# In the mixer, each group's sample step takes its sixteen small products in two runs, by operand height, instead of in turns head by head

## The chip, the cores and the metric

The kernel runs on one core of a Trainium2 chip. The time is the device time of one execution in microseconds (us). A profile of one execution gives the start and duration of every instruction on the engines: PE (TensorE, matmuls), PEld (the weight loads of PE), DVE (VectorE), ACT (ScalarE), POOL (GpSimd), and SP, which issues most DMAs.

## The reference

One step of a streaming encoder: two layers, 512 frames of a new stream (the prompt) and 32 frames of a running stream (the sample), which share all weights. The first layer holds a Mamba-2 mixer, the second a stick-breaking attention; both have two SwiGLU blocks around them. The part that matters here is the mixer's scan, in chunks; the prompt has four chunks of 128 frames in this kernel, the sample is one chunk of 32, and the sample alone starts from a carried state:

```python
cb = jnp.einsum('bign,bjgn->bijg', C_c, B_c)
y_diag = jnp.einsum('bijg,bijge,bjgep->bigep', cb, decay, x_c)
y_off = jnp.einsum('bign,bgepn->bigep', C_c, state) * jnp.exp(a_cs)[..., None]
...
new_state = state * jnp.exp(a_cs[:, -1])[..., None, None] + jnp.einsum(
    'bjgn,bjge,bjgep->bgepn', B_c, w_end, x_c)
return new_state, y_diag + y_off
```

There are 4 groups of 8 heads, 64 columns to a head and 128 states.

## The kernel before

All 544 frames go through the dense products together, as two halves of 272 columns. A dense product is written as three (high and low parts), so that PE runs long rows of `mm` matmuls of 128x128 weights on 272 columns. In the mixer (function `mamba`) the scan of a group g in 0 to 3 and chunk c in 0 to 4 (c = 4 is the sample) is cut into steps that are squeezed in between those dense rows: `turn_x` and `turn_b` (transposes, tiles `xd`, `xw`, `btok`), `decay` and `decay_ab` (tiles `ex`, the decays times C·B, and `ab`, the decays times C), `state` (new state, tile `st`), and `output`.

`output` holds the two products of a head: `xd`ᵀ`ex` (the y_diag term; its operands have as many rows as the chunk has frames: 128, or 32 for the sample) and `st`ᵀ`ab` (the y_off term; 128 rows, one for each state). Both add up in the same place of a PSUM tile `py`. Eight heads share that tile: heads 2t and 2t+1 lie at columns t·128 on, the even one on partitions 0 to 63 (PE's left column half) and the odd one on 64 to 127 (the right half). In the profile's rows the first product is `aux<-ex,xd` and the second `aux<-ab,st`; a form such as 32\*64 is the height and width of the part of PE that the instruction uses. Each of these fp32 products is two instructions on PE.

What follows what on each engine is set by a planner (class `Plan`): each step is a chain that yields requests with a price ("T", 1.2, ... is 1.2 us on PE), and the planner emits whichever can start earliest by its own prices and lags. The engines then keep that order. So a changed price changes the order of everything that the planner places later. The last step of a group's `y` then goes through `gnorms` to the output product (`mm<-yh`, `mm<-yl`).

Of the kernel before, what the change touches and what calls it, by code (L numbers as in the profile page):

```python
# [10 lines left out]
P = 128  # L11
# [4 lines left out]
T = TP + TS  # L16
# [28 lines left out]
NZB, NY, NYH = 1, 2, 4  # L45

RGNORM, RSCAN, RCONV, RGATE, ROUT, RSTEP = 39, 4, 20, 45, 2, 41

FIRST = [0, 1, 2, 3], [0, 1, 2, 3], [0, 1, 2, 3], [0, 1, 2, 3]
GROUPS = [(4, 5), (6, 7)], [(8, 9), (10, 11)], [(12, 13), (14, 15)], [(16, 17), (18, 19), (20, 21)]  # L50
# [126 lines left out]
def v_cost(n):  # L177
    return n / 960.0 + 0.069


def _body(tc, io):
# [17 lines left out]
    V, S, G, TE = (Engine(n, e) for n, e in (("V", nc.vector), ("S", nc.scalar), ("G", nc.gpsimd), ("T", nc.tensor)))  # L199
# [4 lines left out]
    with ExitStack() as ctx:  # L204
# [767 lines left out]
        def mamba(norm, after, ready, ahead):  # L972
            with tc.tile_pool(name="mt", bufs=1, reuse_waits="tile") as tmp, \
# [6 lines left out]
                def aux():  # L980
                    return pa.tile([P, 512], F32, tag="aux", name="aux")
# [8 lines left out]
                got = {}  # L990
# [292 lines left out]
                def before(c):  # L1283
                    return "s" if c == 4 else c - 1
# [33 lines left out]
                def output(g, c):  # L1318
                    off, n = chunks[c]
                    src = off if c < 4 else SOFF  # L1320
                    xs = got["x", g]
                    need = [("ex", g, c), ("xd", g, c), ("xw", g, c), ("cd", g, c)]
                    yield "wait", *need
                    if c > 0:
                        yield "wait", ("st", g, before(c))
                    if c == 0:
                        yield "get", "y"
                        got["y", g] = tmp.tile([P, 4, T], F32, tag="y", name="y", bufs=NY)
                        yield "set", ("y0", g)
                    else:  # L1330
                        yield "wait", ("y0", g)
                    yield "get", "aux"
                    py = aux()
                    xd, ex, ab = got["xd", g, c], got["ex", g, c], got["ab", g, c]

                    def emit(t):
                        for b in range(2):
                            h = 2 * t + b
                            dst = py[64 * b:64 * b + 64, t * P:t * P + n]
                            TE.matmul(dst, xd[:n, h, :], ex[:n, h, :], start=True, stop=c == 0)  # L1340
                            if c > 0:
                                TE.matmul(dst, got["st", g, before(c)][:, h, :], ab[:, h, :], start=False, stop=True)
                    for t in range(4):
                        yield "T", (1.2 if n < P else 0.87) if c else 0.44, lambda: emit(t)
                    yield "set", ("y", g, c)
                    yield "put", "ex"
                    yield "put", "xd"
                    yield "put", "ab"
                    pyv = py[:, :].rearrange("p (t i) -> p t i", t=4)[:, :, :n]
                    yv = got["y", g][:, :, off:off + n]  # L1350

                    def skip(t):
                        V.scalar_tensor_tensor(out=yv[:, t], in0=xs[:, t, src:src + n], scalar=dskip[:, 4 * g + t:4 * g + t + 1], in1=pyv[:, t],
                                               op0=ALU.mult, op1=ALU.add)
                    for t in range(4):
                        yield "W", v_cost(n) + 0.06, lambda: skip(t)
                    yield "put", "aux"
                    yield "set", ("out", g, c)

                def ssd(g):  # L1360
                    yield "wait", "tok", *[("in", g, t) for t in range(6)]
                    if g > 0:
                        yield "wait", ("ex", g - 1, 4), ("xd", g - 1, 4)
                    for c in range(5):
                        yield "spawn", turn_x(g, c)
                        yield "spawn", turn_b(g, c)
                        yield "spawn", decay(g, c)
                        yield "spawn", state(g, c)
                        yield "spawn", output(g, c)
                        if c < 4:  # L1370
                            yield "wait", ("ex", g, c)
                        if c == 2:
                            yield "spawn", old_state(g)
                    yield "wait", *[("out", g, c) for c in range(5)], ("st", g, 4)
                    yield "put", "grp"
# [545 lines left out]
        def space(name, side=None):  # L1921
            st = ExitStack()
            return st, st.enter_context(tc.tile_pool(name=name, bufs=1, reuse_waits="tile", **({"side": side} if side else {})))
# [5 lines left out]
        st, tmp = space("ff")  # L1929
# [34 lines left out]
        st, tmp = space("pl")  # L1964
# [12 lines left out]
        st, tmp = space("ff")  # L1977
# [8 lines left out]
        st, tmp = space("pl")  # L1986
# [145 lines left out]
```

## Time and profile before

| | us |
|---|---|
| median of 3 runs | 2303.37 (2301.47 to 2303.8) |
| the profiled execution | 2301.52 |
| its span, first to last instruction | 2299.8 |
| PE busy | 2267.0 (99%) |
| DVE busy | 1680.0 (73%) |
| ACT busy | 1011.1 (44%) |
| POOL busy | 575.7 (25%) |

An instruction counts as busy from its start to its end, and matmuls overlap, so a busy PE is not PE at its peak: what one matmul costs is read from the time between the starts of two. The profile also gives the clock that was granted to PE in a stretch, as a share of 2.4 GHz: 1.00 is 2.4 GHz and 0.50 is 1.2 GHz.

### The profile page before, as it was taken

To read this page: it belongs to the slowest core of one execution; us is meant where nothing else is said; L and a number is where in the kernel's file an instruction comes from. 1 tells how busy PE (TensorE), PEld (TensorE's weight loads), DVE (VectorE), ACT (ScalarE), POOL (GpSimd) and SP (SyncE) were. 2 spreads that over 40 slices of the span, in tenths; PEclk is the share of its full clock that TensorE was granted. 3 is DMA by queue.
4 is the path that set the end of the run, shared out by engine and by line. 5 is a ranking of instruction groups with operands and counts; after the bars stand their busy time and mean duration, and the time that the engine had idled before them with its cause. 6 is when DMAs were issued, how large, how long until landed. Compare 5 with 4: busy or idle time off the path is not lost.

```text
span 2299.8 us, 42811 instructions
## 1 busy us (share of the span) xinstructions
PE 2267.0 (99%) x17937; PEld 2207.0 (96%) x17937; DVE 1680.0 (73%) x2201; ACT 1011.1 (44%) x1489; POOL 575.7 (25%) x541
## 2 busy tenths in 40 slices
PE   9999999999999999999999999999998999999997
PEld 9999999989899999999999999999985899999997
DVE  7777786679777676777757767778678576777857
ACT  5333334567646353333345533333468353333343
POOL 1221122244324122121221122121234122221224
PEclk9999999999999999999999999999999999999999
DMA  5233323333433232333232423332311132333232
GB/s 170 85 91 106 97 67 90 112 100 94 110 97 99 75 119 79 106 93 106 65 99 91 130 81 104 100 98 65 89 45 56 47 117 86 92 106 97 67 100 76
DMA packets 111537, 213.19 MB, mean 93 GB/s; under 512 B 12400, under 2 KB 33520, under 8 KB 111344
## 3 DMA queue, kind: packets, MB, share of 16 engines
q1 hardware_dynamic: 108464, 204.92, 29.7%
q10 hardware_dynamic: 2880, 5.53, 0.7%
q8 instruction: 141, 2.31, 0.4%
q14 instruction: 52, 0.43, 0.1%
HBM read 204.83 MB, written 5.60 MB: 91 GB/s over the span
## 4 chain that ended last, share of the span: by engine, by line
PE 92%; DVE 4%; ACT 2%; issue 1%; POOL 1%; DMA 1%; SPq 0%; DVEq 0%; ACTq 0%; POOLq 0%
PE mm L193 82%; PE z L193 3%; PE aux L193 3%; PE o L193 1%; PE f L193 1%; PE tr L193 1%; DVE wlo L193 1%; ACT whi L193 1%; DVE xl L193 1%; POOL ab L193 0%; DVE x L193 0%; DVE e L193 0%; DMA wraw<-in_wpg 0%; DVE fu L193 0%; DVE rm L193 0%
## 5 line engine op out<-in xcount | busy, mean ns | idle before, releaser
L193 PE MATMUL mm<-xh,whi 128*128 128x272 f32 x2096 | 513.0, 293 | 2.3 <-DVE x L193 1.0
L193 PE MATMUL mm<-xh,wlo 128*128 128x272 f32 x2096 | 506.2, 289 | 1.8 <-DVE wlo L193 1.8
L193 PE MATMUL mm<-xl,whi 128*128 128x272 f32 x2096 | 507.7, 290 | 0.3 <-DVE xl L193 0.3
L193 PEld LDWEIGHTS mm<-xh,whi 128*128 128x128 f32 x2096 | 358.6, 189 | 10.5 <-issue 7.2
L193 PEld LDWEIGHTS mm<-xh,wlo 128*128 128x128 f32 x2096 | 358.3, 189 | 2.3 <-DVE wlo L193 2.2
L193 PEld LDWEIGHTS mm<-xl,whi 128*128 128x128 f32 x2096 | 358.3, 190 | 0.7 <-DVE xl L193 0.7
L193 ACT ACTIVATE whi<-wraw 128x1024 fp32r<-128x1024 f32 (+3 forms) x215 | 184.2, 858 | 374.5 <-PE mm L193 263.3
L193 PE MATMUL mm<-xfh,whi 128*128 128x272 f32 x1152 | 332.4, 289 | 0.0
L193 PE MATMUL mm<-xfl,whi 128*128 128x272 f32 x1152 | 332.3, 288 | 0.0
L193 PE MATMUL mm<-xfh,wlo 128*128 128x272 f32 x1152 | 332.2, 288 | 0.0
L193 DVE TENSOR_TENSOR wlo<-wraw,whi 128x1024 fp32r<-128x1024 f32 (+3 forms) x252 | 257.0, 1020 | 72.6 <-ACT whi L193 54.6
L193 PE MATMUL mm<-hh,whi 128*128 128x272 f32 x1408 | 291.5, 288 | 0.0
L193 PE MATMUL mm<-hh,wlo 128*128 128x272 f32 x1408 | 291.1, 288 | 0.0
L193 PE MATMUL mm<-hl,whi 128*128 128x272 f32 x1408 | 290.9, 288 | 0.0
L193 ACT ACTIVATE whi<-a 128x1024 fp32r<-128x1024 f32 x127 | 134.9, 1062 | 319.8 <-PE mm L193 214.4
L193 DVE TENSOR_TENSOR wlo<-a,whi 128x1024 fp32r<-128x1024 f32 x145 | 178.4, 1230 | 101.7 <-ACT whi L193 67.2
L193 PEld LDWEIGHTS mm<-hl,whi 128*128 128x128 f32 x1408 | 221.5, 189 | 0.0
L193 PEld LDWEIGHTS mm<-hh,whi 128*128 128x128 f32 x1408 | 221.2, 188 | 0.0
L193 PEld LDWEIGHTS mm<-hh,wlo 128*128 128x128 f32 x1408 | 220.7, 189 | 0.0
L193 PEld LDWEIGHTS mm<-xfh,wlo 128*128 128x128 f32 x1152 | 217.1, 188 | 0.0
L193 PEld LDWEIGHTS mm<-xfl,whi 128*128 128x128 f32 x1152 | 217.1, 188 | 0.0
L193 PEld LDWEIGHTS mm<-xfh,whi 128*128 128x128 f32 x1152 | 217.1, 188 | 0.0
(290 smaller groups left out, 4108.0 us busy)
## 6 DMA issues: line engine op xcount, KB each, us to landing
a<-in_wgu SPq DMA_DIRECT2D x145, 512.0 KB, 3.9
wraw<-in_wd SPq DMA_DIRECT2D x128, 256.0 KB, 2.7
wraw<-in_win SPq DMA_DIRECT2D x41, 512.0 KB, 3.6
wraw<-in_wgu SPq DMA_DIRECT2D x29, 512.0 KB, 3.7
wraw<-in_wd SPq DMA_DIRECT2D x32, 384.0 KB, 3.1
ab<-acs_d SPq DMA_DIRECT2D x16, 512.0 KB, 4.7
wraw<-in_wout SPq DMA_DIRECT2D x16, 512.0 KB, 3.6
wraw<-in_wpg SPq DMA_DIRECT2D x16, 512.0 KB, 3.6
```

Source lines behind the costliest of these rows:

```text
L193: ins = getattr(self.engine, op)(*args, **kw)
```

## The change

For the sample, the step `emit` (a pair of heads, each `ex` product followed by its `ab` product; four such steps) gives way to one step `emit_sample`: all eight heads' `ex` products, then all eight heads' `ab` products. Only the first two of them (t = 0, one in each column half) carry the flag that starts a new sum in the tile. The planner's price for a group's sample step goes from 4 times 1.2 to 1.8. The other four chunks keep their code and prices.

```diff
+TSSD = 0.44, 0.87
...
-                    for t in range(4):
-                        yield "T", (1.2 if n < P else 0.87) if c else 0.44, lambda: emit(t)
+                    def emit_sample():
+
+                        for old in range(2):
+                            for h in range(8):
+                                t, b = divmod(h, 2)
+                                dst = py[64 * b:64 * b + 64, t * P:t * P + n]
+                                if old:
+                                    TE.matmul(dst, got["st", g, before(c)][:, h, :], ab[:, h, :], start=False, stop=True, skip_group_check=True)
+                                else:
+                                    TE.matmul(dst, xd[:n, h, :], ex[:n, h, :], start=t == 0, stop=False, skip_group_check=True)
+                    if n < P:
+                        yield "T", 1.8, emit_sample
+                    else:
+                        for t in range(4):
+                            yield "T", TSSD[c > 0], lambda: emit(t)
```

On PE, at the sample step of group 0, the order before goes on like this for eight heads (one row is one product):

```order
L193 MATMUL mm<-xh_4143,wlo 128x272 x2
L193 MATMUL aux<-ex,xd 64x32
L193 MATMUL aux<-ab,st 64x32
L193 MATMUL aux<-ex,xd 64x32
L193 MATMUL aux<-ab,st 64x32
L193 MATMUL aux<-ex,xd 64x32
```

and now it is this, at the same place between the same dense products:

```order
L195 MATMUL mm<-xl_4144,whi 128x272 x2
L195 MATMUL mm<-xh_4143,wlo 128x272 x2
L195 MATMUL aux<-ex,xd 64x32 x8
L195 MATMUL aux<-ab,st 64x32 x8
L195 MATMUL mm<-xh_4190,whi 128x272 x2
```

The sixteen products have become two runs of eight; up to this place nothing on PE has moved.

Behind that, the planner's order differs. At the sample step of group 2, before, PE had these rows after the last prompt chunk's state product (`xw,btok`), thirty more rows of dense products, and then the sample's products in turns:

```order
L193 MATMUL aux<-C,B 32x32
L193 MATMUL aux<-xw,btok 128x512
L193 MATMUL mm<-yh,whi 128x272 x2
L193 MATMUL mm<-yl,whi 128x272 x2
L193 MATMUL mm<-yh,wlo 128x272 x2
```

Now the sample's products stand three rows of dense products behind it:

```order
L195 MATMUL aux<-xw,btok 128x512
L195 MATMUL mm<-yh,whi 128x272 x2
L195 MATMUL mm<-yl,whi 128x272 x2
L195 MATMUL mm<-yh,wlo 128x272 x2
L195 MATMUL aux<-ex,xd 64x32 x8
L195 MATMUL aux<-ab,st 64x32 x8
```

In the mixer as a whole, the dense rows are broken by scan products 56 times now, 53 times before.

On POOL, whose product `ab<-ab,C` the sample's second run reads, group 2 had this before (the `whi` row is a weight's high part, copied for the dense products):

```order
L193 TENSOR_TENSOR st<-st,fade 128x512
L193 TENSOR_TENSOR xw<-xd,tok 32x512
L193 TENSOR_SCALAR whi<-wraw 128x1024
L193 TENSOR_TENSOR ab<-ab,C 128x256
L193 TENSOR_TENSOR st<-st,fade 128x512
L193 TENSOR_TENSOR yl<-y,yh 128x544
```

and has this now:

```order
L195 TENSOR_TENSOR st<-st,fade 128x512
L195 TENSOR_TENSOR xw<-xd,tok 32x512
L195 TENSOR_TENSOR ab<-ab,C 128x256
L195 TENSOR_TENSOR st<-st,fade 128x512
L195 TENSOR_SCALAR yh<-y 128x544
```

The copy of the weight has left that place of POOL's queue.

## Rows read from the trace of the kernel before

**Rows 1.** Page: busy time of each engine; the chain that ended last, by engine.

```profile
PE 2267.0 (99%) x17937; PEld 2207.0 (96%) x17937; DVE 1680.0 (73%) x2201; ACT 1011.1 (44%) x1489; POOL 575.7 (25%) x541
PE 92%; DVE 4%; ACT 2%; issue 1%; POOL 1%; DMA 1%; SPq 0%; DVEq 0%; ACTq 0%; POOLq 0%
```

**Rows 2.** The mixer: length, busy time of PE, PEld, DVE, ACT, POOL; clock; DMA.

```profile
424.00:760.00 336.00, 332.54 (x2710) 309.75 (x2710) 248.94 (x448) 206.37 (x347) 121.45 (x138) 0.98 0.34 100
```

**Rows 3.** Whom PE waited for, 400 to 860: us in total, times, longest.

```profile
PE aux L193 <- POOL ab L193: 1.2, 2, 0.9
PE aux L193 <- POOL xw L193: 0.9, 1, 0.9
PE aux L193 <- DVE btok L193: 0.8, 1, 0.8
PE mm L193 <- DVE wlo L193: 0.7, 1, 0.7
```

**Rows 4.** PE's order of time, group 2's sample: start, us, instruction, count.

```profile
633.44 0.30 PE L193 MATMUL aux<-ex,xd 32*64 32x32 f32 x2
633.66 0.30 PE L193 MATMUL aux<-ab,st 128*64 128x32 f32 x2
...
636.87 0.30 PE L193 MATMUL aux<-ab,st 128*64 128x32 f32 x2
637.10 0.52 PE L193 MATMUL mm<-yh,whi 128*128 128x272 f32 x2
```

**Rows 5.** The same, cut fine: first pair's second matmul, its two weight loads.

```profile
633.52 0.22 PE L193 MATMUL aux<-ex,xd 32*64 32x32 f32 x1
633.43 0.13 PEld L193 LDWEIGHTS aux<-ex,xd 32*64 32x64 f32 x1
633.49 0.13 PEld L193 LDWEIGHTS aux<-ex,xd 32*64 32x64 f32 x1
```

**Rows 6.** PE cut fine (0.02 and 0.01 us), then whole: runs of one form.

```profile
1766.03 0.33 PE L193 MATMUL o<-an,vt 32*64 32x128 f32 x2
543.14 0.33 PE L193 MATMUL aux<-ex,xd 128*64 128x128 f32 x2
543.14 1.09 PE L193 MATMUL aux<-ex,xd 128*64 128x128 f32 x16
```

**Rows 7.** Stretches, PE alone: length, busy time and instructions, granted clock, DMA.

```profile
489.00:492.40 3.40, 3.40 (x31) 1.00 0.30 107
492.40:495.81 3.41, 3.41 (x16) 0.50 0.59 159
495.81:499.20 3.39, 3.39 (x29) 1.00 0.00 0
633.44:637.10 3.66, 3.66 (x33) 1.00 0.36 140
637.10:640.50 3.40, 3.40 (x29) 1.00 0.51 153
584.56:587.97 3.41, 3.41 (x15) 0.50 0.58 154
```

**Rows 8.** PE and POOL in order of time, sample steps of groups 0 and 3.

```profile
487.78 0.30 PE L193 MATMUL aux<-ex,xd 32*64 32x32 f32 x2
488.94 0.30 PE L193 MATMUL aux<-ab,st 128*64 128x32 f32 x2 [0.86 <-POOL ab L193]
492.38 0.82 PE L193 MATMUL mm<-xh,whi 128*128 128x272 f32 x2
487.75 1.14 POOL L193 TENSOR_TENSOR ab<-ab,C 128x256 f32<-128x256 f32 x1 [2.14 <-DVE fade L193]
741.26 0.30 PE L193 MATMUL aux<-ex,xd 32*64 32x32 f32 x2
741.85 0.30 PE L193 MATMUL aux<-ab,st 128*64 128x32 f32 x2 [0.29 <-POOL ab L193]
745.44 0.82 PE L193 MATMUL mm<-xh,whi 128*128 128x272 f32 x2
```

## The prediction

> **What bounds the kernel now.** Read the page first: PE is busy for 99% of the span, and the chain of work that ended last is PE's for 92% [rows 1]. So a microsecond taken from PE's stream is a microsecond of the whole, as long as PE does not then wait for another engine. The edit lies in the mixer, so the view by stretches comes next: from 424 to 760 PE is busy for 332.5 of 336 us, DVE for 249, POOL for 121 [rows 2]. The view of waits says the same: the four longest releasers held PE for 3.6 us from 400 to 860, one wait never for more than 0.9 [rows 3]. PE is the bound, and what counts is how densely its matmuls start.
>
> The view in order of time then shows how thin the sample steps are. In group 2, the first `ex` product starts at 633.44, its `ab` product at 633.66, and so on through sixteen pairs of instructions; the dense products go on at 637.10 [rows 4]. That is 3.66 us for 32 matmuls of 32 columns, 0.23 a pair. Cut fine, the pair's second matmul starts at 633.52, 0.08 behind its first, and their weight loads 0.06 apart [rows 5]. The other 0.15 of each 0.23 passes before an instruction of the other height (32\*64 against 128\*64) may start: sixteen changes from one height to the other, 2.4 us of the 3.66.
>
> Where the height stays the same, PE shows none of this, and more. The attention's `o<-an,vt` has the very form 32\*64: two of its matmuls have started within 0.02 us of 1766.03 [rows 6]. They are of two heads in PE's two column halves, which run side by side. The same holds for `ex` products of a prompt chunk: two have started within 0.01 us, and sixteen take 1.09 from the first start to the last end [rows 6]. In the sample's turns this can't be seen, since each change of height stands between one head and the next.
>
> Last, the view by stretches with the granted clock. PE runs at 2.4 GHz nearly everywhere, but after the sample of group 0, from 492.40, it runs at 1.2 GHz (0.50) for 3.41 us and starts 16 matmuls where 29 start in the 3.39 us after [rows 7]. The 3.40 us ahead of the fall held nothing but the sample's thin products (31 instructions). The same fall stands behind the samples of group 1, at 584.56 [rows 7], and of group 3, a third time. Behind group 2's it does not: 1.00 during and after [rows 7].
>
> **The change, part by part.**
>
> *Sixteen changes of height become two a group.* I cost the new step from its parts. Each run is eight heads, four to a column half, so eight matmuls in each half. With the halves side by side, a run is seven steps from the first start to the last. A step is bounded above by the 0.08 between the two matmuls of a pair, and below by the 0.06 between their weight loads [rows 5]. Add 0.15 for the change between the runs and 0.15 for the one back to dense products: 1.14 to 1.42 us. I take 1.25, since in a run the next loads can go ahead, as they can't behind a change. Groups 1 and 2 then save 3.66 − 1.25 = 2.4 each.
>
> Group 0 waits: its second product could not start until 488.94, since POOL's `ab` (from 487.75, for 1.14) was late [rows 8]. Now all eight `ex` products run under that wait, and the eight `ab` products follow from 488.94 on, in 0.47 + 0.15. The step ends at 489.56, not 492.38: 2.8 saved. Group 3's wait of 0.29 [rows 8] vanishes under its first run: 741.26 + 1.25 = 742.5 instead of 745.44, 2.9 saved. Sum: 2.4 + 2.4 + 2.8 + 2.9 = 10.5 us; with 1.42 in place of 1.25 it is 9.9, with 1.14 it is 11.
>
> *The clock.* A step of 1.25 us with dense products on both sides is far from the 3.40 us of thin products that preceded the fall in group 0, and shorter than group 2's 3.66, which cost nothing. I take it that the three falls go. Each lost 29 − 16 = 13 dense matmuls, which take 3.39 / 29 = 0.12 us each at the full clock: 1.6 us, together 4.8.
>
> *The new order.* From group 1 on, the planner places everything anew. The dense rows are broken 56 times instead of 53; a break costs at most the two changes at its edges, 0.3, and I put 0.2 on each, 0.6 together. No other instruction is added or removed on PE, and no DMA; some copies of weights and products of `y` change hands between POOL, ACT and DVE, and on SP the loads of `ab` and of weights trade places by one or two in groups 1 and 2. None of PE's waits named a DMA [rows 3]. Waits are the unknown. PE reaches its later products some 15 us earlier in 336, while DVE's 249 and POOL's 121 us of work stay, so they have cover; but group 2's sample now stands three dense rows (0.75 us) behind the last prompt chunk's state product instead of thirty. What must be ready then is POOL's `ab` (1.14) behind POOL's step of the state, and PE, in order, would hold the dense products behind it. Below, all 3.6 us of waits vanish; above, each group gets a wait as long as group 0's two together (0.86 and the 0.9 for `xw`), which is 3.5 us more than now. I take 2 more.
>
> **Sum.** The profiled execution took 2301.52, of which 1.7 lie around the span. 2301.52 − 10.5 − 4.8 + 0.6 + 2 = 2288.8. The median of the runs lies 1.85 above the profiled execution, so 2290.7 us for a median: 12.7 us or 0.55% faster. About 0.2% (4.6 us) is what a measurement of this kernel can tell from no change.
>
> **The rivals.**
>
> *The halves don't overlap.* With 32 rows, the two halves share the same rows of PE, and heads could still go one behind another: 15 steps of 0.08 in each run, 2.7 us a group. That saves 1.0 in each of groups 1 and 2, 1.9 in group 0, 1.5 in group 3 (part of their runs lies under the waits), 5.4 in all, and the median is 2295.8. For it speaks that the first matmuls of a pair do stand 0.08 apart; against it the two `an,vt` matmuls within 0.02 us at the same height [rows 6]. The Trainium skill (TensorE: Matmul & The Clock Gate, Part 3, "The mechanism") says that weight loads overlap matmuls in flight only where the row groups differ; here they don't differ, so by that rule this rival would be the outcome, at 2295.8. The `an,vt` rows speak against it, so I give it one chance in ten.
>
> *The clock still falls.* The sample is followed or preceded by other sparse work (group 0 also stands still for 1.2 us until `ab` is there). If all three falls stay, 4.8 come back: 2295.5. For it: I know only three cases with a fall and one without. 15 in 100.
>
> *The new order eats the gain.* Waits of 8 us or more over the mixer instead of 2: about 2297 to 2300. For it: everything from group 1 on is placed anew by prices that are not the chip's. Against it: the price of 1.8 is nearer to my 1.25 than 4.8 was to 3.66, and PE waited little under the worse prices. 10 in 100.
>
> *Slower.* One mechanism would do it: POOL's queue. If each sample step finds `ab` late because POOL is still at a prompt chunk's state, with the dense products held behind it on PE, a wait costs what POOL has in front. To end over 2308 (0.2% slower), PE's waits must grow by more than 19 us, almost 5 us a group against the 0.9 now. POOL is idle for almost two thirds of the mixer [rows 2]. 3 in 100.
>
> *The change does not do what it says.* If the 0.15 were not due to the height, but to `ab` adding into the place that `ex` has just written, it would be paid in the prompt chunks too, and the sample's runs would lose it anyway, since no product adds onto the one just before it. So this ends near the forecast, and I give it no chance of its own. That the time doesn't move at all for a reason that I can't see: 2 in 100.
>
> **How the numbers follow.** The forecast has 60 in 100, and its own range, from the bounds of the runs and waits, is 2285 to 2295. The clock's fall (15) and the halves one by one (10) reach to 2295.8; with a bit of both, to 2298. Below, waits that vanish (−5.6) and the lower price of the runs (−0.5) give 2284.6; I leave a little room under that. The range is 2283 to 2298. Faster by over 0.2% (below 2298.8): the forecast, the clock, the halves, and half of the eaten gain: 90 in 100. The same: 7. Slower: 3.
>
> **What would show each step.** In order of time, a sample step should show sixteen `ex` matmuls and then sixteen `ab` matmuls, each run within 0.8 us, and at most 1.5 us from the first start to the next dense product. If the starts come singly, 0.06 to 0.08 apart, the halves don't overlap. By stretches, the clock should stay at 1.00 behind every sample. In the view of waits, PE's sum over the mixer should stay under 8 us. The prediction is wrong if the steps are as short as said and the time has hardly moved: then another engine held PE back, and the view of waits names it.

## The result, and the profile of the changed kernel

The changed kernel takes 2289.85 us (median of 4 runs, 2288.41 to 2291.31), beside 2303.59 for the kernel before on the same chip: a ratio of 0.9931 [0.9919, 0.9943], 0.7% faster; the two medians themselves stand 13.7 us apart, 0.6%. The forecast was 2290.7. The profiled execution took 2290.30, its span is 2288.5.

The page's busy times and its chain by engine, which answer to [rows 1]:

```profile
PE 2252.2 (98%) x17937; PEld 2194.9 (96%) x17937; DVE 1677.5 (73%) x2204; ACT 1015.0 (44%) x1492; POOL 569.8 (25%) x539
PE 89%; DVE 4%; issue 3%; ACT 2%; POOL 2%; DMA 1%; SPq 0%; DVEq 0%; ACTq 0%; POOLq 0%
```

PE has the same 17937 instructions and is busy for 14.8 us less; it is still the bound.

PE in order of time, at the samples of groups 0, 1 and 2 (start, us, instruction, count, and in brackets the wait ahead of it):

```profile
489.98 0.65 PE L195 MATMUL aux<-ex,xd 32*64 32x32 f32 x16
491.14 0.66 PE L195 MATMUL aux<-ab,st 128*64 128x32 f32 x16 [0.51 <-POOL ab L195]
491.73 0.52 PE L195 MATMUL mm<-xh,whi 128*128 128x272 f32 x2
...
582.63 0.65 PE L195 MATMUL aux<-ex,xd 32*64 32x32 f32 x16 [1.50 <-DVE y L195]
583.21 0.66 PE L195 MATMUL aux<-ab,st 128*64 128x32 f32 x16
583.80 0.33 PE L195 MATMUL aux<-ident,B 128*128 128x128 f32 x1
...
629.95 0.65 PE L195 MATMUL aux<-ex,xd 32*64 32x32 f32 x16 [0.79 <-DVE ex L195]
630.84 0.66 PE L195 MATMUL aux<-ab,st 128*64 128x32 f32 x16 [0.23 <-POOL ab L195]
631.43 0.52 PE L195 MATMUL mm<-yh,whi 128*128 128x272 f32 x2
```

From the first start to the next instruction, group 1's step takes 583.80 − 582.63 = 1.17 us, group 0's 1.75 and group 2's 1.48, since `ab` is late between the runs there; group 3's takes 1.18. A run lasts 0.65; one matmul of it lasts 0.22 [rows 5], so sixteen start within 0.43, seven steps of about 0.06 in each half. The next run starts 0.58 after the first: the other 0.15 is the change of height. Cut to 0.02 us, at the start of group 1's run, first PE and then its weight loads:

```profile
582.63 0.24 PE L195 MATMUL aux<-ex,xd 32*64 32x32 f32 x2 [1.50 <-DVE y L195]
582.60 0.19 PEld L195 LDWEIGHTS aux<-ex,xd 32*64 32x64 f32 x3 [1.69 <-issue]
```

Two matmuls of 0.22 lie within 0.24, so they started within 0.02; three loads of 0.13 [rows 5] lie within 0.19. The halves run side by side.

The stretches behind the four samples, PE alone (length, busy time and instructions, granted clock, DMA), which answer to [rows 7]:

```profile
491.73:495.14 3.41, 3.41 (x31) 1.00 0.57 172
583.89:587.30 3.41, 3.41 (x22) 1.00 0.80 253
631.43:634.84 3.41, 3.41 (x31) 1.00 0.59 167
736.02:739.43 3.41, 3.41 (x31) 1.00 0.42 165
```

The clock stays at 2.4 GHz behind every one. By stretches with all engines, a piece of the start and the mixer, which answers to [rows 2]; then the waits of PE from 400 to 860, which answer to [rows 3]:

```profile
8.40:11.80 3.40, 3.33 (x14) 3.01 (x15) 3.04 (x6) 3.29 (x7) 0.00 (x0) 0.50 1.02 372
424.00:760.00 336.00, 330.80 (x2814) 310.53 (x2813) 253.71 (x463) 214.81 (x356) 119.09 (x137) 1.00 0.36 104
```

```profile
PE aux L195 <- DVE y L195: 1.5, 1, 1.5
PE aux L195 <- DVE xd L195: 1.2, 1, 1.2
PE aux L195 <- POOL xw L195: 0.9, 1, 0.9
PE aux L195 <- DVE ex L195: 0.8, 1, 0.8
PE aux L195 <- POOL ab L195: 0.7, 2, 0.5
PE mm L195 <- DVE wlo L195: 0.7, 1, 0.7
```

In the mixer PE starts 2814 instructions in the 336 us that held 2710, at a clock of 1.00 instead of 0.98. Three waits are new, on DVE's `y`, `xd` and `ex`; the whole view comes to 5.8 us instead of 4.1.

### The profile page after: what moved, and what is told of

It reads as the page before. It is cut to its first block, busy times and chain, and to the rows that moved or that the text cites. A ratio compares the mean times of both kernels' runs of the same rounds, so it can differ in the third digit from the quotient of the medians.

```text
span 2288.5 us, 42806 instructions
## 1 busy us (share of the span) xinstructions
PE 2252.2 (98%) x17937; PEld 2194.9 (96%) x17937; DVE 1677.5 (73%) x2204; ACT 1015.0 (44%) x1492; POOL 569.8 (25%) x539
## 4 chain that ended last, share of the span: by engine, by line
PE 89%; DVE 4%; issue 3%; ACT 2%; POOL 2%; DMA 1%; SPq 0%; DVEq 0%; ACTq 0%; POOLq 0%
PE mm L195 80%; PE z L195 3%; PE o L195 1%; PE aux L195 1%; PE f L195 1%; PE tr L195 1%; DVE wlo L195 1%; POOL ab L195 1%; ACT whi L195 1%; DVE xl L195 1%; DVE x L195 0%; POOL st L195 0%; DMA wraw<-in_wpg 0%; ACT ex L195 0%; DVE fu L195 0%
```

## The experiments

Each kernel is the changed one with the edit shown. The kernel before took 2306.85 us beside the first four, 2306.67 beside the kernel with each run twice and beside the last one, and 2305.85 beside the other four. The theory is the prediction's: the steps give 10.5 us and the clock 4.8, and the new order costs some 2 to 3. The rivals put the gain into the new order, the 0.15 into something other than the height, or the fall of the clock into something other than the thin products.

**The products in runs, everything else in the old order.** The planner sees the old four requests.

```diff
-                        yield "T", 1.8, emit_sample
+                        for k in range(4):
+                            yield "T", 1.2, emit_sample if k == 0 else lambda: None
```

> The new order of the sample's products, with the planner's old price (four requests of 1.2 us), so that every other instruction on every engine keeps the order of the kernel before. Theory (the gain is in the sample steps and in the clock behind them): steps of 1.2 us plus what is left of the waits, no fall of the clock behind a sample, PE's waits in the mixer about 3.5 us as before; 2303.6 - 10.5 - 4.8 = 2288 us, 1 to 3 us under the changed kernel. Rival (the gain comes from the new order that the planner made): about 2303, as before. A run within 2 us of 2290 but with the same waits as the changed kernel would mean that the new order neither costs nor gives.

It took 2292.77, ratio 0.9939 [0.9926, 0.9952]: most of the gain is there without the new order. The steps take 1.76, 1.65, 1.17 and 1.18. But it is not the 1 to 3 us under the changed kernel that the theory expected; the runs lie at 2290.62 to 2294.49, level with those or a little above. The old order has a price of its own. PE, then DVE, then PE's stretch, ahead of a prompt chunk's products in group 1:

```profile
580.62 0.41 PE L195 MATMUL mm<-xh,wlo 128*128 128x272 f32 x2
583.75 1.62 PE L195 MATMUL aux<-ex,xd 128*64 128x128 f32 x14 [2.72 <-DVE y L195]
```

```profile
581.62 1.22 DVE L195 TENSOR_TENSOR ex<-ex,cb 128x1024 f32<-128x1024 f32 x1 [3.69 <-ACT ex L195]
582.76 0.24 DVE L195 SCALAR_TENSOR_TENSOR y<-xs,vecs,aux 128x32 f32<-128x32 f32 x1
582.92 0.68 DVE L195 COPY st<-aux 128x512 f32<-128x512 f32 x1
583.52 0.23 DVE L195 SCALAR_TENSOR_TENSOR y<-xs,vecs,aux 128x32 f32<-128x32 f32 x1
```

```profile
583.90:587.30 3.40, 3.40 (x21) 0.51 0.54 159
```

The sample's sums are read by DVE's `y` instructions, which in the old order stand behind and between other work; PE, now early, waits 2.72 us for the tile, and 0.2 us into the prompt chunk's products its clock falls. From group 0's sample to the end of group 3's this execution takes 248.6 us (488.14 to 736.75), the changed kernel's 246.0 (489.98 to 736.02).

**The old turns in the new order.** The price stays 1.8.

```diff
-                        yield "T", 1.8, emit_sample
+                        yield "T", 1.8, lambda: [emit(t) for t in range(4)]
```

> The old turns head by head, with the new price of 1.8 us, so that every other instruction keeps the order of the changed kernel. Theory: steps of 3.66 us, the clock falls behind two to four of the four samples, and the new order's own cost of about 2 us in waits and breaks; 2303.6 + 2 = 2305.5 us, between 2302 and 2309. Rival (the planner's new order saves by itself): 2290 to 2297.

It took 2311.53, ratio 1.0021 [1.0012, 1.003]: slower than before. So the new order gives nothing by itself; it costs 4.7 us as long as the step is thin. PE's order of time in group 2, and two of its four stretches with a fall:

```profile
641.65 0.30 PE L195 MATMUL aux<-ex,xd 32*64 32x32 f32 x2
641.88 0.42 PE L195 MATMUL aux<-ab,st 128*64 128x32 f32 x2
642.23 0.42 PE L195 MATMUL aux<-ex,xd 32*64 32x32 f32 x2
```

```profile
641.87:652.11 10.24, 10.24 (x53) 0.50 0.31 88
754.51:761.34 6.83, 6.83 (x35) 0.50 0.13 47
```

All four samples now have a fall, and it begins inside the step: from 641.88 a pair takes 0.35 instead of 0.23. The falls last longer than the 3.41 of the profile of before: with 6.8 from 491.69 and 10.2 from 587.26 they come to 34.1 us, beside 10.2 there. PE's waits are 6.9 us, 2.8 more. How the 4.7 divides between the waits and the longer falls is not shown: the kernel before has falls of 6.8 us too, in its second execution (further down).

**The column halves one behind the other.**

```diff
-                            for h in range(8):
+                            for h in (0, 2, 4, 6, 1, 3, 5, 7):
```

> The changed kernel, with the heads of each run taken even ones first, then odd ones (0, 2, 4, 6, 1, 3, 5, 7): as many changes of height, but neighbours share a column half. Theory (halves run side by side only where neighbours alternate): each run is 15 steps of 0.055 to 0.08 us, a step of a group 2.0 to 2.7 us against 1.17, the whole 3 to 6 us longer than the changed kernel, 2293 to 2296 us. Rival (two loads of 64 columns in a row cost no more in one half than in two, so that the step is bounded by the count of matmuls alone): steps of 1.2 us and 2290 us.

It took 2292.16, ratio 0.994 [0.9927, 0.9952]. PE in order of time, at the start of group 2's step and in group 3's:

```profile
630.28 1.40 PE L195 MATMUL aux<-ex,xd 32*64 32x32 f32 x16 [0.79 <-DVE ex L195]
...
738.73 0.91 PE L195 MATMUL aux<-ex,xd 32*64 32x32 f32 x16
739.57 0.91 PE L195 MATMUL aux<-ab,st 128*64 128x32 f32 x16
740.41 0.52 PE L195 MATMUL mm<-xh,whi 128*128 128x272 f32 x2
```

Group 3's step takes 1.68, not the 2.0 to 2.7 expected. The sixteen start within 0.91 − 0.22 = 0.69; one behind the other they would need fifteen steps of 0.06, 0.9. The rows do not name the half, but this fits only if the second half's matmuls start beside the last ones of the first half, though they stand behind them in the order. Alternating heads still gains 0.25 a run. Two samples have a fall of the clock here, with steps hardly longer than the changed kernel's. At group 1 it starts at 582.7, behind the step (1.65) and a wait of 1.49 for `y`. At group 2, by stretch:

```profile
630.45:633.85 3.40, 3.40 (x35) 0.50 0.46 88
```

The clock falls 0.17 us into the step, after the first few of its matmuls. So here the step can hardly have made it fall. Ahead of it stand a wait of 0.79, three dense products and a chunk's state product; but the changed kernel has the same work and the same wait at that place, and no fall in either of its two executions, so this does not settle it either.

**Turns, but both products of one height.** The first product is replaced by a second `st`·`ab` product.

```diff
-                        for old in range(2):
-                            for h in range(8):
...
+                        for h in range(8):
+                            t, b = divmod(h, 2)
+                            dst = py[64 * b:64 * b + 64, t * P:t * P + n]
+                            for old in range(2):
+                                TE.matmul(dst, got["st", g, before(c)][:, h, :], ab[:, h, :], start=t == 0 and not old, stop=old == 1, skip_group_check=True)
```

> The changed kernel's plan, with the old turns head by head, but the first product of a head is replaced by a second one of the carried state with ab, so that both are 128 rows high (the sample's y_diag term is left out). Theory (the 0.15 us belongs to the change of height): no such gap inside the step; 16 slots of 0.055 us in each half, 0.9 to 1.3 us a step, the whole within 3 us of the changed kernel, 2288 to 2293 us. Rival (the gap comes from adding onto the place just written): steps of 3.66 us and 2302 to 2309 us.

It took 2291.95, ratio 0.9938 [0.9926, 0.9949]. PE, group 3:

```profile
735.65 1.15 PE L195 MATMUL aux<-ab,st 128*64 128x32 f32 x32 [0.52 <-POOL ab L195]
736.73 0.52 PE L195 MATMUL mm<-xh,whi 128*128 128x272 f32 x2
```

Thirty-two matmuls take 1.08, in turns head by head and each second one adding onto the sum just written. Fifteen steps of 0.06 in each half are 0.9, so no 0.15 is left between one product and the next: it has gone with the change of height. The 0.15 that remains of the 1.08 stands at the end, where 128\*64 gives way to the dense 128\*128: a change of width, at one height.

**Two heads' first products, then their second ones:** eight changes of height.

```diff
-                        for old in range(2):
-                            for h in range(8):
...
+                        for t in range(4):
+                            for old in range(2):
+                                for h in (2 * t, 2 * t + 1):
```

> The changed kernel, with the sixteen products pair by pair: two heads' first products, then the same two heads' second products, four times; eight changes of height in a step (the one at its end counted) instead of two. Theory (0.15 us for each change, 0.08 for the two matmuls side by side before it): 8 x 0.23 = 1.84 us a step with no wait, against 1.17; the whole some 2 to 3 us longer than the changed kernel of the same call, and no fall of the clock behind a sample. Rival (what the old turns lost was the halves side by side, not the change of height): a step of 1.2 to 1.3 us.

It took 2298.24, ratio 0.9969 [0.9958, 0.9981]. PE's order of time in group 1, and two stretches:

```profile
581.74 0.30 PE L195 MATMUL aux<-ex,xd 32*64 32x32 f32 x4 [1.50 <-DVE y L195]
581.97 0.31 PE L195 MATMUL aux<-ab,st 128*64 128x32 f32 x4
...
583.62 0.33 PE L195 MATMUL aux<-ident,B 128*128 128x128 f32 x1
```

```profile
584.30:587.70 3.40, 3.40 (x12) 0.51 1.03 203
632.00:635.40 3.40, 3.21 (x31) 0.51 0.37 118
```

The step takes 1.88, 0.235 for each change, as expected: four matmuls of two heads cost what two of one head cost before. But the clock falls behind group 1's step and from 632.04 inside group 2's (from 631.29), which was not expected: a step of half the old length, with a wait of 1.50 ahead of it in group 1, does not keep it up.

**Each run three times, or twice.** The sums start anew each time, so only the work grows.

```diff
-                        for old in range(2):
+                        for old in (0, 1, 0, 1, 0, 1):
```

> The changed kernel, with the two runs of a sample step made three times over (the first matmul of each time starts the sum anew, so the values stay): 96 matmuls in about 3.5 us, as long as the old step of 3.66 us with 32. Theory (the clock fell because the old steps were thin in time, not because they were small or long): no fall of the clock behind a sample; steps 2 x 1.17 = 2.3 us longer, the whole 9 us longer than the changed kernel. Rival (small matmuls for three and more us let the clock fall however dense they are): falls behind two to four samples, 12 to 16 us longer.

It took 2306.19, ratio 1.0004 [0.9996, 1.0013], 16.9 more than the changed kernel in the same comparison. PE, group 3, and its stretches:

```profile
747.69 0.65 PE L195 MATMUL aux<-ex,xd 32*64 32x32 f32 x16
...
751.22 0.63 PE L195 MATMUL mm<-xh,whi 128*128 128x272 f32 x2
```

```profile
747.69:751.21 3.52, 3.52 (x97) 1.00 0.48 149
751.50:754.90 3.40, 3.40 (x17) 0.50 0.24 82
```

The step (96 matmuls; the row counts one more, which still ran at its start) is as dense as in the changed kernel and as long as the old one, and the clock falls behind it; groups 1 and 2 have such a fall late in the step. The theory that only thinness in time makes the clock fall has fallen here. Group 0's fall is of another kind: it starts at 488.63, ahead of the step at 489.38. PE's order up to there is the changed kernel's, so the edit did not make it; the wait of 0.93 for `xw`, over since 486.31, stands in the changed kernel too. With two turns (`for old in (0, 1, 0, 1)`):

> The changed kernel, with the two runs of a sample step made twice: 64 matmuls in about 2.3 us where nothing is waited for. Made three times (3.5 us) the clock fell at every sample; once (1.2 us) behind none. Theory (the clock falls where small matmuls and waits together last long enough, however dense): one or two falls, at groups 1 and 2, where PE waits 1.5 and 0.8 us ahead of the step, and none at group 3, where it waits for nothing; 4 us for the steps and 2 to 3 for the falls, 0.996 of the kernel before. Rival (it is the count of small matmuls): no fall, 0.995, or falls at group 3 too.

It took 2297.16, ratio 0.9961 [0.9948, 0.9973], with falls at groups 1, 2 and 3, none at group 0. Group 3's:

```profile
740.70:742.40 1.70, 1.70 (x49) 1.00 0.81 243
742.40:745.80 3.40, 3.40 (x32) 0.50 0.30 114
```

It begins inside the step, after 1.7 us of small products, which the expectation did not hold.

**A lower price.**

```diff
-                        yield "T", 1.8, emit_sample
+                        yield "T", 1.2, emit_sample
```

> The changed kernel, with the planner's price for the sample step at 1.2 us, which is what the step takes in the changed kernel's profile, in place of 1.8; everything behind the first sample is placed anew. Theory (the waits that PE has left come from an order made with wrong prices): PE's waits in the mixer fall from about 5.8 to 3 to 4 us, the whole 0 to 3 us shorter than the changed kernel. Rival (any new order trades waits at random): between 3 us shorter and 5 us longer, with other waits in place of those gone.

It took 2288.68, ratio 0.9924 [0.991, 0.9937], 0.7 us under the changed kernel beside it, which can't be told from it. PE's waits come to 3.8 us instead of 5.8: with the price next to the measured 1.2, those for `y`, `xd` and `ex` are gone and one of 1.2 for ACT's `xs` is new, but the gain is too small to show.

**The two kernels again.** The changed one:

> The changed kernel once more, for the same chip and call as the three others: 0.993 of the kernel before, PE's waits and steps as in its first profile, no fall of the clock behind a sample.

It took 2289.34, ratio 0.9934 [0.992, 0.9947], with the same steps, the same waits and no fall behind a sample in the profiled execution. One of its five runs took 2297.22 at a mean granted clock of 0.992; the other four, and the first four of the changed kernel, had 0.996 or 0.997. That run has no trace, so where it lost the clock is not known. The kernel before:

> The kernel before once more, for one look at its clock: falls behind two to four of the four sample steps, and behind group 2's this time if the place of the fall differs from one execution to the next; steps of 3.66 us wherever the clock stays up.

One run, 2308.3. PE alone during group 1's sample, and behind group 2's:

```profile
583.07:586.73 3.66, 3.66 (x33) 1.00 0.19 72
639.31:646.14 6.83, 6.83 (x32) 0.50 0.26 77
```

Again three falls (the others from 492.54 and 748.53), but now at group 2, beginning late in its step, and not at group 1: the same step, in the same order, brings a fall in one execution and not in another. And each lasts 6.83 us here, where each lasted 3.41 in the first profile.

## Why the prediction was right

**The steps.** Forecast 10.5 us, measured 10.5, in part by luck, since two small errors cancel. The old steps took 4.60, 3.67, 3.67 and 4.17, together 16.1; the new ones 1.75, 1.17, 1.48 and 1.18, together 5.6. The step taken as 1.25 is 1.17, near the lower bound of 1.14, since the steps in a run are as long as those between weight loads (0.06), not those between matmuls of a pair (0.08) [rows 5]. Groups 0 and 2 are longer by 0.6 and 0.3, with `ab` late between the runs; group 0's wait was foretold, group 2's was not part of the 10.5. The three ways to take part of the edit agree: eight changes take 0.235 each with their matmuls, turns at one height leave 1.08, and the runs alone, in the old order, already give 0.6%.

**The height.** The kernel with both products of one height shows it: no gap, though each second product adds onto the first. There both have the same operands, too; that operands that differ cost nothing is seen in the prompt chunks of the kernel before, where `ex` and `ab` products alternate at one height:

```profile
620.69 0.44 PE L193 MATMUL aux<-ab,st 128*64 128x128 f32 x4
620.91 0.44 PE L193 MATMUL aux<-ex,xd 128*64 128x128 f32 x4
```

Four matmuls of 128 columns take 0.22, with no 0.15 between. But the prediction's name for the cost is too narrow. The last of its sixteen changes, from `ab` to the dense products, keeps the height of 128 and only widens the form from 64 to 128, and it costs the same: group 1's `ab` run starts at 583.21 and the next product at 583.80, 0.59 like the 0.58 between the runs. What costs 0.15 is a change of the form, in height or in width. The Trainium skill (TensorEngine Tiling (Array Packing), Key Properties) states that a change of the tiling mode drains the engine; these traces agree, at 0.15 us a change.

**The halves.** Two matmuls have started within 0.02 us in the first cut of a run, and a run is as long as seven steps. The Trainium skill (TensorE: Matmul & The Clock Gate, Part 3, "The mechanism") has weight loads overlap matmuls in flight only where the row groups differ; here the rows are the same and the columns differ, and the loads and the matmuls overlap. As the prediction read that rule, the step would be 2.7, and it is 1.17: the measurement decides.

**The clock.** Forecast −4.8, for three falls behind samples that go; they are gone, in both profiled executions of the changed kernel, and 1.00 stands behind every sample. That the stretch from group 0's sample to the end of group 3's has shrunk by 11.6 us fits: 10.5 of steps and two falls of 1.6 inside it, less 2.2 of waits outside the steps; most of the third fall lies behind it, though it began at 744.98, inside group 3's step. The unprofiled runs agree as a whole: the mean granted clock was 0.991 to 0.994 in all 41 runs of the kernel before that stood beside the experiments, and 0.996 or 0.997 in eight of the nine of the changed one. The outcome is right, but its ground was too sure. "Far from" a fall was argued from the length of the thin products alone. The clock fell at two samples of four in the kernel with the halves apart (steps of 1.65 to 2.01 wherever the clock stayed up), at two with eight changes of form (1.9 with no wait inside), at three with each run twice and at all four with each run thrice; and in the kernel before, the same step of 3.67 does or doesn't bring a fall. So density does not keep the clock up, and a short step does not rule a fall out: behind a wait, a step only half a microsecond longer had one. With the shortest steps, 1.06 to 1.76 us, there was none at twenty samples in five executions: the changed kernel twice, the lower price, the one height and the old order with runs, whose one fall stands at a prompt chunk. But two falls began just at a step's start or ahead of it, at places where the changed kernel does the same work just before and kept its clock. What decides whether the clock falls in an execution stays open; no run here changes the waits alone, and each experiment was profiled once. The size was luck as well: the 4.8 was read from an execution of the kernel before whose falls last 3.41 us, and in the other one each lasts 6.83, with 2308.3 us for the whole.

**The new order.** Forecast +2 of waits and +0.6 of breaks. The waits rose by 1.7; without those for `ab`, which lie inside the steps and so in the 10.5 already, they went from 2.9 to 5.1, by 2.2. The breaks were not measured apart. The wait foretold for group 2 is there: PE stands for `ex` (0.8) and `ab` (0.2) at its sample. The longest new one is for `y`, which the prediction did not name. The rival that sought the gain in the new order has fallen: by itself it makes the kernel 4.7 us slower.

**The sum.** The profiled execution came to 2290.30, where 2288.8 was worked out. It has one fall at the very start, from 8.40, that the profile of before lacks; it was there in the second execution of the changed kernel and of the kernel before too, and group 0's sample stands at 489.98 instead of 487.78 [rows 8]. In the attention it is the other way round: the profile of before has two falls there, from 1734.85 and 1823.60, and the changed one only the one from 1732.11. Neither place is part of the change, and they nearly cancel. The sum for the median, 2290.7, is 0.85 above what was measured; that it comes so near is in part luck, since the median of the kernel before was 2303.59 in the first comparison and 2305.85 to 2306.85 in the later ones, and the changed kernel's gain 13.7 and 16.5 us.

## What to carry to other kernels

Order small matmuls by the form of PE that they use, here by the height of their operands, with the column halves alternating: a change cost 0.15 us here and a matmul in a run about 0.03. Tell the planner the new price, since in the old order the faster step ran into readers that came too late; but look at whether the old order with the new step is already as good. A fall of 3.4 us behind a stretch of small products cost 1.6 us, so shortening such a stretch can return more than its own length; whether a given execution has the fall could not be foretold here, so compare many runs and more than one profile.

## What the hardware showed unexpectedly

The order within a run is not strict across column halves: with all left heads first, a run of sixteen took 0.69 us from first to last start, less than the 0.9 of one by one. Density does not hold the clock: 96 small matmuls in 3.52 us at 1.00 were followed by 3.40 us at 0.50. A change of width at one height, from 128\*64 to 128\*128, costs as much as a change of height, 0.15 us.
